# Weight sums of a down projection by transfers in DRAM, moved from the attention phase to the up phase, in a hybrid encoder block on one core

## The chip, the core and the metric

The kernel runs on one core of a Trainium2 chip. The core has five engines, each with an instruction queue of its own that is worked off in order: PE (TensorE, matrix products), DVE (VectorE), ACT (ScalarE), POOL (GpSimd) and SP (SyncE, which here only issues transfers). Sixteen DMA engines move the data of all queues. A transfer that SP or POOL issues is started when the instruction's turn comes and its semaphores are satisfied; until then everything behind it on that queue stands still.

The metric is the device time of one execution in microseconds. Nothing is computed on the host but the layout of the inputs.

## The reference, cut to what matters

One encoder layer with 512 tokens and a model width of 2048, in float32:

```
mod = silu(c) @ w_ada + b_ada;  sh1, sc1, gt1, sh2, sc2, gt2 = split(mod, 6)
h = rms_norm(x, g_mix) * (1 + sc1) + sh1
xr, yr, q, k, v, f = split(h @ w_in)
y_rec = recurrent group(conv, gates, scan over time) * gelu(yr)
y_att = attention of 8 heads with a forget bias, q and k normalised per head
x = x + gt1 * (concat(rms_norm(y_rec), rms_norm(y_att)) @ w_out)
h2 = rms_norm(x, g_ffn) * (1 + sc2) + sh2
gate, up = split(h2 @ w_up)
x = x + gt2 * ((silu(gate) * up) @ w_down)
```

`w_up` is 2048 x 11264 and `w_down` 5632 x 2048. The row gt2 (2048 values) scales the last sum.

## The kernel before, in words

Weights come from HBM in float32. Each weight tile, and each activation, is split into a rounded part (ACT) and a remainder (DVE), and each product is made of three matmuls (high by high, high by low, low by high). The program is written with a tile framework: its scheduler orders the instructions of each engine by their place in the source and by the priorities given (`tc.high_priority(offset=...)` moves a block forward in the order), as soon as data and a buffer are there in its own model of time. The order is fixed when the kernel is built; what the chip then does is to wait, queue by queue. `tc.issue_after(ins)` puts what the block issues behind `ins` on the queue of `ins`, and adds no wait.

The stages follow one another:

- input projections, from 0 to about 190 us;
- the heads (`head_evac`, `attention`, `rec_pair`): the projection of head h+1 runs on PE while hooks between its steps do the attention of head h, a part of the recurrent group and some columns of `w_ada`. Each head's statistics `ss` go through POOL (`rms_rstd`, lines 277 and 280), because the power -1/2 is taken there; `norm` on DVE waits for it, the transposes of q and k on PE wait for `norm`;
- the output projection `wo0` to `wo3` (from about 670 us), then two groups of the up projection, `up0` and `up1` (from 850 us), with the rstd of the new x through POOL;
- the up phase (`for f in range(2 * STD, FT)`, 40 values of f): seven products per f in place of eight, from sums and differences of quarters (a Strassen scheme). Each f has two chunks, c = 0 and 1; a chunk loads 1 MB of weights by two transfers on SP (`fast_chunk`, line 1019). The loads of c = 0 use tag `raw`, those of c = 1 tag `raw2`, with two buffers each. After each chunk, with n = 2 (f - 4) + c, the source calls `gt2_piece` (while n < 64) and `sum2` (for n even, while n < 66). `keep_act` writes the activations to DRAM tiles `td`;
- the down phase: the seven products of a second scheme in four phases (`PHASES`): products 4 and 5, 1 and 7, 6, 2 and 3. Each phase runs over 11 blocks q (`NQ`). `dn_chunk` loads for each product the weight block (`dn_load`, line 1080), 1 MB as two transfers with two buffers of `raw` and two of `raw2`, and the activations (line 1092) into pages `tl`, splits both, and `dn_mm` issues 24 matmuls per q and product.

Some products take sums of weight blocks. `wdn[0..3]` are the four quarters of `w_down`, by q. Product 6 takes `wdn[0] + wdn[2] + wdn[3]`, product 3 the same plus `wdn[1]`; others take a sum of two, made on DVE (line 1099) after the loads. The sum of three is made in DRAM by `sum2`: for n = 0 SP copies `wdn[0, q]` into `s2d[q]` (line 966), for n = 1 and 2 POOL issues two transfers of half a block each that add `wdn[2, q]` and `wdn[3, q]` onto it (line 970). Each waits for the one before it on the same half. Product 3 loads `s2d[q]` and adds the other product's block `wdn[1, q]` on DVE.

Pages are tiles of 128 x 512 from pools by tag: 32 of "h", 16 of "b", 16 of "c", 4 of "d". A page is free for the next user when its last reader is done. In the up phase the transformed inputs T hold all "h" pages and some of the others. In the down phase `tl` and `th` come from "h". In phase 3 the products of the last two q of product 2 are held back (`hold`, lines 1100 to 1109) so that the outputs can be finished one by one; their 16 pages come from "c".

`gt2_spread` brings gt2 from a column layout (`mods[GT2]`, 128 x 16) into rows spread over all partitions: PE transpose, ACT copy, a store of 16 rows to `gt2d` in DRAM (line 1133), and four spreading loads into pages `gt2b` (line 1137), called in phase 2 after q = 2. `finish` (lines 1140 to 1146) loads a piece of x, multiplies and adds on DVE, and stores the outputs that are complete after phase 2; `last_out` does the rest in phase 3.

Of the kernel before, what the change touches and what calls it, by code (L numbers as in the profile page):

```python
# [8 lines left out]
F32 = mybir.dt.float32  # L9
# [5 lines left out]
P = 128  # L15
# [48 lines left out]
def block_kernel(ctx, tc, xT, crow, adaT, vecs, bfr, w1, wyr, wqkv0, wqkv, wgate, wout, wup0, wups, wdn, outT):  # L64
# [16 lines left out]
    def page(name, tag, shape=None):  # L81
        return pgp.tile(shape or [P, S], F32, tag=tag, name=name, bufs=TAGS[tag])

    def acc(name):
        return psa.tile([P, S], F32, tag="acc", name=name)
# [875 lines left out]
        nc.sync.dma_start(out=td[1][q][:, 1, ks], in_=w[:, :HS])  # L961
        nc.sync.dma_start(out=td[2][q][:, 0, ks], in_=w[:, HS:])

    def sum2(q, n):
        if n == 0:
            nc.sync.dma_start(out=s2d[q], in_=wdn[0, q])
        else:
            for i in range(2):
                cs = slice(i * 1024, (i + 1) * 1024)
                nc.gpsimd.dma_start(out=s2d[q][:, cs], in_=wdn[n + 1, q, :, cs], accum_op=ALU.add)  # L970

    def up_out(gi, ps, bup, fs):
        for f in fs:
# [36 lines left out]
    def fast_chunk(f, c):  # L1010

        nm = f"uq{f}_{c}"
        with tc.high_priority(offset=AHEAD):
            if c:
                raw = bp.tile([P, 2048], F32, tag="raw2", name=nm + "r")
            else:
                raw = wp.tile([P, 2048], F32, tag="raw", name=nm + "r", bufs=RAW)
            for i in range(2):
                nc.sync.dma_start(out=raw[:, i * 1024:(i + 1) * 1024], in_=wups[f - 2 * STD, c, :, i * 1024:(i + 1) * 1024])
            blocks = raw.rearrange("p (b m) -> p b m", b=4)  # L1020
            hi, lo = wsplit(raw[:, :1024], 1024, nm + "a")
            out = [(4, hi[:, :512], lo[:, :512]), (1, hi[:, 512:], lo[:, 512:])]
            hi, lo = page(nm + "ch", "d"), page(nm + "cl", "d")
            nc.scalar.activation(R(hi), blocks[:, 3], AF.Copy)
            nc.vector.tensor_sub(R(lo), blocks[:, 3], hi)
            out.append((2, hi, lo))
            nc.vector.tensor_add(blocks[:, 0:3:2], blocks[:, 0:2], blocks[:, 2:3].broadcast_to([P, 2, 512]))  # L1027
            nc.vector.tensor_add(blocks[:, 1], blocks[:, 1], blocks[:, 0])  # L1028
            hi, lo = wsplit(raw[:, :1024], 1024, nm + "s")
            out += [(5, hi[:, :512], lo[:, :512]), (6, hi[:, 512:], lo[:, 512:])]  # L1030
            nc.vector.tensor_add(blocks[:, 3], blocks[:, 3], blocks[:, 1])  # L1031
            hi, lo = wsplit(raw[:, 1024:], 1024, nm + "t")
            out += [(7, hi[:, :512], lo[:, :512]), (3, hi[:, 512:], lo[:, 512:])]
        return out
# [5 lines left out]
    for f in range(2 * STD, FT):  # L1040
        ps = [bank(f + 1, b, f"uf{f}p{b}") for b in range(4)]
        m = {p: ps[b][:, h * HS:(h + 1) * HS] for p, (b, h) in where.items()}
        for c in range(2):
            for p, hi, lo in fast_chunk(f, c):
                for k in range(4):
                    th, tl = T[p][c * 4 + k]
                    ks = slice(k * P, (k + 1) * P)
                    for n, (w, x) in enumerate(((hi, th), (hi, tl), (lo, th))):
                        first, last = c + k + n == 0, c == 1 and k == 3 and n == 2
                        nc.tensor.matmul(m[p], lhsT=R(w[:, ks]), rhs=R(x), start=first and p in opens, stop=last,  # L1050
                                         skip_group_check=True)
            if f == 2 * STD and c == 0:
                up_last()
            n = 2 * (f - 2 * STD) + c
            if n < 4 * KT:
                gt2_piece(n)
            if n < 6 * NQ and n % 2 == 0:
                sum2(n // 6, n // 2 % 3)
        g, u = page(f"ug{f}", "c"), page(f"uu{f}", "c")
        w1_, w2_ = (ap_.tile([P, S], F32, tag="x", name=f"uw{f}_{i}", bufs=2) for i in range(2))  # L1060
        two = lambda t: t.rearrange("p (a b) -> p a b", a=2)
        twice = lambda t: t.unsqueeze(1).broadcast_to(halves)
        nc.scalar.activation(w1_[:, lo_half], m[1], AF.Copy)
        nc.vector.tensor_add(two(g), two(ps[0]), twice(w1_[:, lo_half]))
        nc.vector.tensor_sub(two(w2_), twice(g[:, hi_half]), two(ps[1]))
        nc.vector.tensor_add(g[:, hi_half], m[3], w2_[:, lo_half])
        nc.vector.tensor_sub(u[:, lo_half], m[4], w2_[:, hi_half])
        nc.vector.tensor_sub(u[:, hi_half], m[5], w2_[:, hi_half])
        nc.scalar.activation(g, g, AF.Silu)
        nc.vector.tensor_mul(g, g, u)  # L1070
        keep_act(g, f)

    PHASES = (((4, 3, 1), (5, 2, 0)), ((1, 0, 0), (7, 2, 1)), ((6, -1, 0),), ((2, 1, 0), (3, -1, 1)))

    def dn_load(tag, blk, q, nm):
        pool = wp if tag == "raw" else bp
        raw = pool.tile([P, 2048], F32, tag=tag, name=nm, bufs=RAW)
        src = s2d[q] if blk < 0 else wdn[blk, q]
        for i in range(2):
            nc.sync.dma_start(out=raw[:, i * 1024:(i + 1) * 1024], in_=src[:, i * 1024:(i + 1) * 1024])  # L1080
        return raw

    def dn_chunk(ph, q, hold=False):
        prods = PHASES[ph]
        out = {p: [] for p, _, _ in prods}
        with tc.high_priority(offset=AHEAD):
            raws, ts = [], []
            for n, (p, blk, ix) in enumerate(prods):
                nm = f"dq{p}_{q}"
                raws.append(dn_load("raw2" if n or (len(prods) == 1 and q % 2) else "raw", blk, q, nm + "r"))  # L1090
                tl, th = page(nm + "tl", "h"), page(nm + "th", "h")
                nc.sync.dma_start(out=tl, in_=td[ph][q][:, ix])
                nc.scalar.activation(R(th), tl, AF.Copy)
                nc.vector.tensor_sub(R(tl), tl, th)
                ts.append((th, tl))
            for n, (p, blk, ix) in enumerate(prods):
                nm, raw = f"dq{p}_{q}", raws[n]
                if n:
                    nc.vector.tensor_add(raw, raw, raws[0])
                for k in range(2):  # L1100
                    if hold and n == 0:
                        w = []
                        for i in range(2):
                            src = raw[:, (2 * k + i) * S:(2 * k + i + 1) * S]
                            hi, lo = page(f"{nm}h{k}{i}", "c"), page(f"{nm}l{k}{i}", "c")
                            nc.scalar.activation(R(hi), src, AF.Copy)
                            nc.vector.tensor_sub(R(lo), src, hi)
                            w.append((hi, lo))
                    else:
                        hi, lo = wsplit(raw[:, k * 1024:(k + 1) * 1024], 1024, f"{nm}w{k}")  # L1110
                        w = [(hi[:, i * S:(i + 1) * S], lo[:, i * S:(i + 1) * S]) for i in range(2)]
                    ks = slice(k * HS, (k + 1) * HS)
                    out[p].append((w, ts[n][0][:, ks], ts[n][1][:, ks]))
        return out
# [10 lines left out]
    gt2b = []  # L1125

    def gt2_spread():
        pt = acc("gt2p")
        nc.tensor.transpose(out=pt[:KT, :P], in_=mods[GT2], identity=ident)
        row = page("gt2r", "d")  # L1130
        nc.scalar.activation(row[:KT, :P], pt[:KT, :P], AF.Copy)
        gd = drp.tile([KT, P], F32, name="gt2d")
        nc.sync.dma_start(out=gd, in_=row[:KT, :P])
        gv = gd.rearrange("(a k) p -> a k p", k=4)
        for a in range(4):
            g = page(f"gt2b{a}", "h")
            nc.sync.dma_start(out=g.rearrange("p (k m) -> p k m", k=4), in_=gv[a:a + 1].broadcast_to([P, 4, P]))
            gt2b.append(g)

    def finish(y, tt, a, nm, out=True):  # L1140
        xt = page(nm + "x", "d")
        nc.sync.dma_start(out=xt, in_=x1t[tt, a])
        nc.vector.tensor_mul(y, y, gt2b[a])
        nc.vector.tensor_add(y, y, xt)
        if out:
            nc.sync.dma_start(out=outT[tt][:, a * S:(a + 1) * S], in_=y)

    def last_out(ps, b, z, tt, nm):
        i = b % 2
# [13 lines left out]
    for ph, prods in enumerate(PHASES):  # L1163
# [4 lines left out]
        for q in range(NQ):  # L1168
# [4 lines left out]
            for p, cells in out.items():  # L1173
                for k, cell in enumerate(cells):
                    dn_mm(ps[p], *cell, ALL, q + k == 0, q == NQ - 1 and k == 1)
            if ph == 2 and q == 2:
                gt2_spread()
        if ph == 0:
            q4, q5 = copies(ps[4], "q4_"), copies(ps[5], "q5_")
# [5 lines left out]
                    nc.vector.tensor_add(x_[b], ps[7][b], q5[b])  # L1185
                    nc.vector.tensor_add(q4[b], ps[7][b], q4[b])
        elif ph == 2:
            v = [page(f"dv{b}", "h") for b in range(4)]
            with tc.high_priority(offset=EVAC):
                for b in range(4):  # L1190
                    nc.vector.tensor_add(v[b], ps[6][b], q1[b])
# [80 lines left out]
```

## Time and profile before

| | us |
|---|---|
| median of 3 runs | 2217.03 |
| lowest and highest | 2216.04, 2217.51 |
| the profiled execution | 2223.3 |
| its span, from the first to the last instruction | 2221.6 |
| PE busy in the span | 2064.6 (93%) |
| DVE busy | 1742.0 (78%) |
| ACT busy | 951.7 (43%) |
| POOL busy | 68.3 (3%) |

The profile is one execution, so sums made from it go by its own 2223.3 us, 6.3 above the median of the runs. The page's slices are 55.5 us each; a digit is the busy share in tenths. In lists of waits, a row names who waited, for whom, and then the sum in us, how often, and the longest. A row of a timeline gives start, length, engine (SPq is SP's transfer queue), line, operation, output and input. A transfer's row shows its issue; the time to landing is given separately. Names such as dq_5r or uq_0r leave out buffer numbers, so that dq_5r stands for the weights of q = 5 of any product.

### The profile page before, as it was taken

Reading aid. Unit: us, or ns where it says so; the run is one execution under the profiler, and the core shown is the slowest. Engines: PE = TensorE matmul, PEld = TensorE weight load, DVE = VectorE, ACT = ScalarE, POOL = GpSimd, SP = SyncE. Lnnn points to the kernel's source line nnn. Section 1 sums busy time; section 2 is a strip of 40 time slices with the busy share of each in tenths; the row PEclk is TensorE's granted clock in tenths of the full one; section 3 lists DMA queues with packets and bytes.
Section 4 is the critical chain, followed back from the end, with each engine's and each line's share of the span. In section 5 each row is a group of like instructions: output and inputs, shape, how many; then the busy total and the mean of one; then the engine's idle time right before and its main releaser. Section 6 shows DMA issues by size and latency. Waiting matters only on the chain.

```text
span 2221.6 us, 32358 instructions
## 1 busy us (share of the span) xinstructions
PE 2064.6 (93%) x12538; PEld 1873.0 (84%) x12538; DVE 1742.0 (78%) x2573; ACT 951.7 (43%) x1316; POOL 68.3 (3%) x81
## 2 busy tenths in 40 slices
PE   8999935679999999999999999999999999997898
PEld 6789835568887888889999999999999988886777
DVE  8899513459768867999988888888888877774798
ACT  4433412447644324544444444444444455443443
POOL 0000121110001000000000000000000000000000
PEclk9999967779999999999999999999999999998999
DMA  9989899986766876345644334343334576765684
GB/s 341 332 307 301 283 243 233 263 244 224 239 234 230 284 265 218 106 146 188 194 130 134 131 118 138 119 134 126 129 128 133 172 253 240 245 233 203 221 287 171
DMA packets 163372, 462.14 MB, mean 208 GB/s; under 512 B 17457, under 2 KB 42465, under 8 KB 158946
## 3 DMA queue, kind: packets, MB, share of 16 engines
q1 hardware_dynamic: 156882, 437.00, 57.8%
q0 software_dynamic: 6336, 23.07, 6.0%
q8 instruction: 98, 1.61, 0.3%
q14 instruction: 56, 0.46, 0.1%
HBM read 424.33 MB, written 70.28 MB: 223 GB/s over the span
## 4 chain that ended last, share of the span: by engine, by line
PE 72%; DMA 12%; DVE 11%; issue 3%; POOL 1%; ACT 1%; SPq 1%; DVEq 0%; POOLq 0%; ACTq 0%
DMA s2d<-in_wdn 5%; PE w1p L231 4%; PE dn6p L231 3%; PE dn7p L231 3%; PE dn1p L231 3%; PE dn5p L231 3%; DMA ada<-in_adaT 2%; PE dn4p L231 2%; PE yr1p L231 2%; PE up0p L231 2%; PE wo3p L231 2%; PE wo2p L231 2%; PE wo1p L231 2%; PE yr0p L231 2%; PE wo0p L231 2%
## 5 line engine op out<-in xcount | busy, mean ns | idle before, releaser
L153 DVE SCALAR_TENSOR_TENSOR ada<-ada,c_b 128x1024 f32<-128x1024 f32 x96 | 116.1, 1219 | 107.5 <-DMA ada<-in_adaT 107.3
L226 ACT ACTIVATE uq_0sh<-uq_0r 128x1024 fp32r<-128x1024 f32 x40 | 42.4, 1060 | 116.2 <-DVE uq_0r L1028 112.1
L227 DVE TENSOR_TENSOR uq_0al<-uq_0r,uq_0ah 128x1024 fp32r<-128x1024 f32 x40 | 49.0, 1224 | 39.7 <-ACT uq_0ah L226 38.6
L226 ACT ACTIVATE uq_1sh<-uq_1r 128x1024 fp32r<-128x1024 f32 x40 | 42.4, 1060 | 86.9 <-DVE uq_1r L1028 86.5
L227 DVE TENSOR_TENSOR uq_0tl<-uq_0r,uq_0th 128x1024 fp32r<-128x1024 f32 x40 | 48.9, 1224 | 32.1 <-ACT uq_0th L226 32.1
L226 ACT ACTIVATE uq_0ah<-uq_0r 128x1024 fp32r<-128x1024 f32 x40 | 42.4, 1060 | 69.0 <-DMA td<-tw 25.5
L226 ACT ACTIVATE uq_1ah<-uq_1r 128x1024 fp32r<-128x1024 f32 x40 | 42.4, 1061 | 57.0 <-issue 57.0
L227 DVE TENSOR_TENSOR uq_0sl<-uq_0r,uq_0sh 128x1024 fp32r<-128x1024 f32 x40 | 49.0, 1225 | 16.3 <-ACT uq_0sh L226 16.3
L226 ACT ACTIVATE uq_0th<-uq_0r 128x1024 fp32r<-128x1024 f32 x40 | 42.4, 1060 | 43.9 <-DVE uq_0r L1031 3.2
L181 DVE SCALAR_TENSOR_TENSOR gt<-gt,c_b 128x512 f32<-128x512 f32 x64 | 43.8, 686 | 18.9 <-DMA gt<-in_adaT 18.6
L226 ACT ACTIVATE uq_1th<-uq_1r 128x1024 fp32r<-128x1024 f32 x40 | 42.4, 1059 | 33.7 <-PE uf31p L1050 1.3
L227 DVE TENSOR_TENSOR uq_1tl<-uq_1r,uq_1th 128x1024 fp32r<-128x1024 f32 x40 | 48.9, 1224 | 9.6 <-ACT uq_1th L226 9.6
L231 PE MATMUL w1p<-hph,w1h 128*128 128x512 f32 x128 | 47.6, 400 | 5.8 <-ACT hph L372 5.8
L231 PE MATMUL w1p<-hpl,w1h 128*128 128x512 f32 x128 | 51.0, 398 | 0.1
L231 PE MATMUL w1p<-hph,w1l 128*128 128x512 f32 x128 | 50.8, 397 | 0.0
L1027 DVE TENSOR_TENSOR uq_0r<-uq_0r 128x1024 f32<-128x1024 f32 x40 | 48.7, 1218 | 0.0
L513 DVE TENSOR_TENSOR qk<-qk,ss 128x512 f32<-128x512 f32 x16 | 10.7, 689 | 48.5 <-POOL ss L280 48.5
L227 DVE TENSOR_TENSOR uq_1sl<-uq_1r,uq_1sh 128x1024 fp32r<-128x1024 f32 x40 | 48.7, 1218 | 0.0
L227 DVE TENSOR_TENSOR uq_1al<-uq_1r,uq_1ah 128x1024 fp32r<-128x1024 f32 x40 | 48.6, 1216 | 0.0
L1027 DVE TENSOR_TENSOR uq_1r<-uq_1r 128x1024 f32<-128x1024 f32 x40 | 48.6, 1214 | 0.0
L541 PE MATMUL s<-qkT,qkT 128*128 128x128 f32 (+3 forms) x64 | 25.7, 505 | 22.1 <-DVE nm L546 17.1
L520 PE MATMUL qkt<-ident,qk 128*128 128x128 f32 x64 | 10.1, 310 | 38.4 <-DVE qk L513 38.4
(12773 smaller groups left out, 8254.0 us busy)
## 6 DMA issues: line engine op xcount, KB each, us to landing
ada<-in_adaT SPq DMA_DIRECT2D x128, 512.0 KB, 5.6
uq_1r<-in_wups SPq DMA_DIRECT2D x80, 512.0 KB, 4.3
uq_0r<-in_wups SPq DMA_DIRECT2D x80, 512.0 KB, 4.7
s2d<-in_wdn POOLq DMA_DIRECT2D x44, 512.0 KB, 12.1
adf<-in_adaT SPq DMA_DIRECT2D x32, 512.0 KB, 6.0
gt<-in_adaT SPq DMA_DIRECT2D x64, 256.0 KB, 3.3
x<-in_xT SPq DMA_DIRECT2D x32, 256.0 KB, 5.9
w1r<-in_w SPq DMA_DIRECT2D x32, 256.0 KB, 5.8
```

Source lines behind the costliest of these rows:

```text
L153: nc.vector.scalar_tensor_tensor(out=t, in0=t, scalar=1.0, in1=cs, op0=ALU.mult, op1=ALU.mult, accum_out=ac)
L181: nc.vector.scalar_tensor_tensor(out=t, in0=t, scalar=1.0, in1=c_b[:, r * S:(r + 1) * S], op0=ALU.mult, op1=ALU.mult, accum_out=gt2_acc[:, ...
L226: nc.scalar.activation(R(hi[:, :n]), raw_ap, AF.Copy)
L227: tail_lo.append(nc.vector.tensor_sub(R(lo[:, :n]), raw_ap, hi[:, :n]).ins)
L231: nc.tensor.matmul(ps, lhsT=R(l), rhs=R(r), start=start, stop=stop)
L513: nc.vector.tensor_tensor(z, z, ss[:, 4 * a:4 * a + 4].unsqueeze(2).broadcast_to([P, NT, P]), ALU.mult)
L520: nc.tensor.transpose(out=pt[:, t * P:(t + 1) * P], in_=z[:, t, :], identity=ident)
L541: nc.tensor.matmul(ps[:, :n], lhsT=qT[:, bs], rhs=kT[:, :n], start=True, stop=False)
L1027: nc.vector.tensor_add(blocks[:, 0:3:2], blocks[:, 0:2], blocks[:, 2:3].broadcast_to([P, 2, 512]))
```

## The change

The copies are tied to SP's queue behind the last weight load that the up phase's source has issued so far; a second DRAM tile `s4d` per q takes the sum of four; POOL adds `s2d` onto it. Where before n even called `sum2`, now n = 3, 4, 5, 6 of each six call `sums24`. Product 3 loads `s4d`, and its sum on DVE goes. `gt2_spread` writes `gt2d` straight from the column layout by a transfer with the two axes exchanged, and is called in phase 0. The pages of `gt2b` and `dv` go from "h" to "c", those of the held products from "c" to "h". The stores of `finish` are issued by POOL.

```
+    s4d = [drp.tile([P, 2048], F32, name=f"s4d{q}") for q in range(NQ)]
+    up_loads = []
+
+    def dram_sum(out, src):
+        for i in range(2):
+            cs = slice(i * 1024, (i + 1) * 1024)
+            nc.gpsimd.dma_start(out=out[:, cs], in_=src[:, cs], accum_op=ALU.add)
+
+    def sums24(q, n):
         if n == 0:
-            nc.sync.dma_start(out=s2d[q], in_=wdn[0, q])
+            with tc.issue_after(up_loads[-1]):
+                nc.sync.dma_start(out=s2d[q], in_=wdn[0, q])
+                nc.sync.dma_start(out=s4d[q], in_=wdn[1, q])
+        elif n < 3:
+            dram_sum(s2d[q], wdn[n + 1, q])
         else:
-            for i in range(2):
-                cs = slice(i * 1024, (i + 1) * 1024)
-                nc.gpsimd.dma_start(out=s2d[q][:, cs], in_=wdn[n + 1, q, :, cs], accum_op=ALU.add)
+            dram_sum(s4d[q], s2d[q])
...
-                nc.sync.dma_start(out=raw[:, i * 1024:(i + 1) * 1024], in_=wups[f - 2 * STD, c, :, i * 1024:(i + 1) * 1024])
+                ld = nc.sync.dma_start(out=raw[:, i * 1024:(i + 1) * 1024], in_=wups[f - 2 * STD, c, :, i * 1024:(i + 1) * 1024])
+            up_loads.append(ld.ins)
...
-            if n < 6 * NQ and n % 2 == 0:
-                sum2(n // 6, n // 2 % 3)
+            if 3 <= n < 3 + 6 * NQ and n % 6 in (3, 4, 5, 0):
+                sums24((n - 3) // 6, (n - 3) % 6)
...
-    PHASES = (((4, 3, 1), (5, 2, 0)), ((1, 0, 0), (7, 2, 1)), ((6, -1, 0),), ((2, 1, 0), (3, -1, 1)))
+    PHASES = (((4, 3, 1), (5, 2, 0)), ((1, 0, 0), (7, 2, 1)), ((6, -2, 0),), ((2, 1, 0), (3, -4, 1)))
...
-        src = s2d[q] if blk < 0 else wdn[blk, q]
+        src = {-2: s2d, -4: s4d}[blk][q] if blk < 0 else wdn[blk, q]
...
-                if n:
+                if n and blk >= 0:
                     nc.vector.tensor_add(raw, raw, raws[0])
...
-                            hi, lo = page(f"{nm}h{k}{i}", "c"), page(f"{nm}l{k}{i}", "c")
+                            hi, lo = page(f"{nm}h{k}{i}", "h"), page(f"{nm}l{k}{i}", "h")
...
     def gt2_spread():
-        pt = acc("gt2p")
-        nc.tensor.transpose(out=pt[:KT, :P], in_=mods[GT2], identity=ident)
-        row = page("gt2r", "d")
-        nc.scalar.activation(row[:KT, :P], pt[:KT, :P], AF.Copy)
         gd = drp.tile([KT, P], F32, name="gt2d")
-        nc.sync.dma_start(out=gd, in_=row[:KT, :P])
+        nc.sync.dma_start(out=gd.rearrange("k p -> p k"), in_=mods[GT2])
         gv = gd.rearrange("(a k) p -> a k p", k=4)
         for a in range(4):
-            g = page(f"gt2b{a}", "h")
+            g = page(f"gt2b{a}", "c")
...
-            nc.sync.dma_start(out=outT[tt][:, a * S:(a + 1) * S], in_=y)
+            nc.gpsimd.dma_start(out=outT[tt][:, a * S:(a + 1) * S], in_=y)
...
-            if ph == 2 and q == 2:
+            if ph == 0 and q == 2:
                 gt2_spread()
...
-            v = [page(f"dv{b}", "h") for b in range(4)]
+            v = [page(f"dv{b}", "c") for b in range(4)]
```

More of the change, by code (lines that the diff above doesn't have):

```diff
@@ L962, in keep_act @@
         nc.sync.dma_start(out=td[2][q][:, 0, ks], in_=w[:, HS:])
-    def sum2(q, n):
-        if n == 0:
-            nc.sync.dma_start(out=s2d[q], in_=wdn[0, q])
-        else:
-            for i in range(2):
-                cs = slice(i * 1024, (i + 1) * 1024)
-                nc.gpsimd.dma_start(out=s2d[q][:, cs], in_=wdn[n + 1, q, :, cs], accum_op=ALU.add)
+    s4d = [drp.tile([P, 2048], F32, name=f"s4d{q}") for q in range(NQ)]
[5 more added lines that the diff above has]
+    def sums24(q, n):
+        if n == 0:
+            with tc.issue_after(up_loads[-1]):
[3 more added lines that the diff above has]
+            dram_sum(s2d[q], wdn[n + 1, q])
+        else:
+            dram_sum(s4d[q], s2d[q])
     def up_out(gi, ps, bup, fs):
```

## The prediction, made before the changed kernel was run

> **What bounds the kernel now.** I read the page first, then the busy time by stretches, the list of waits, and the order of the instructions on POOL and SP.
>
> ```profile
> span 2221.6 us, 32358 instructions
> ...
> PE   8999935679999999999999999999999999997898
> ...
> q1 hardware_dynamic: 156882, 437.00, 57.8%
> q0 software_dynamic: 6336, 23.07, 6.0%
> ```
>
> PE is the bound, except in one hole (slices 4 to 8, some 220 to 500 us) and two dents near the end. Those are the places where the change can win; where PE is full it can only lose. The stretches, cut at the points that matter below (columns: length, PE busy, PEld, DVE, ACT, POOL, granted clock, DMA share, GB/s):
>
> ```profile
> 188.83:241.05 52.22, 47.47 (x261) 43.62 (x260) 45.26 (x101) 17.88 (x37) 2.28 (x3) 0.97 0.87 285
> 241.05:486.38 245.33, 146.18 (x698) 132.88 (x696) 93.12 (x174) 74.62 (x140) 42.74 (x51) 0.76 0.98 251
> 486.38:623.69 137.31, 133.68 (x722) 120.98 (x721) 115.19 (x211) 93.87 (x164) 8.24 (x7) 1.00 0.72 235
> 808.00:886.00 78.00, 78.00 (x384) 65.73 (x383) 56.49 (x92) 30.85 (x45) 2.11 (x2) 1.00 0.65 229
> 977.00:1745.00 768.00, 768.00 (x6402) 768.00 (x6402) 663.38 (x908) 321.31 (x381) 0.00 (x0) 1.00 0.43 140
> 2006.63:2080.38 73.75, 60.13 (x254) 49.21 (x254) 37.22 (x38) 26.93 (x30) 0.00 (x0) 0.88 0.61 206
> 2080.38:2221.60 141.22, 126.54 (x540) 101.55 (x539) 124.75 (x143) 57.04 (x69) 0.00 (x0) 0.97 0.68 231
> ```
>
> The first three are cut at POOL's per-head statistics (ss, one per attention head), so their lengths are head times:
>
> ```profile
> 241.05 0.63 POOL L277 TENSOR_SCALAR ss<-ss 128x8 f32<-128x8 f32 x1 [49.86 <-DVE ss L506]
> ...
> 325.81 0.20 POOL L277 TENSOR_SCALAR ss<-ss 128x8 f32<-128x8 f32 x1
> ...
> 413.48 0.20 POOL L277 TENSOR_SCALAR ss<-ss 128x8 f32<-128x8 f32 x1
> ...
> 486.38 1.09 POOL L277 TENSOR_SCALAR ss<-ss 128x8 f32<-128x8 f32 x1 [15.03 <-DVE ss L506]
> ...
> 623.69 1.10 POOL L277 TENSOR_SCALAR ss<-ss 128x8 f32<-128x8 f32 x1 [41.24 <-DVE ss L506]
> ```
>
> Heads 2, 3 and 4 follow after 84.8, 87.7 and 72.9 us, 245.3 in all. The next three take 137.3, that is 45.8 each, with slightly more PE, DVE and ACT instructions. What lies only in the slow stretch are the weight sums s2d, which nothing ties to the down projection that reads them:
>
> ```profile
> L970 POOL DMA_DIRECT2D s2d<-in_wdn x44: 802/823/1216, 257.4 to 470.5; - x44
> ...
> DMA to landing us min/median/max: 7.8/12.1/21.0
> ```
>
> ```profile
> POOL s2d L970 <- DMA s2d<-in_wdn: 137.7, 24, 14.0
> ...
> DVE qk L513 <- POOL ss L280: 48.5, 8, 25.4
> ...
> PE qkt L520 <- DVE qk L513: 38.4, 1, 38.4
> ...
> PE dn6p L231 <- ACT dq_3th L1093: 13.6, 1, 13.6
> ...
> PE dn2p L231 <- ACT dq_0th L1093: 6.6, 1, 6.6
> ```
>
> They hurt twice. The accumulating transfers stand in POOL's queue ahead of ss and wait there for their predecessors (137.7 us); DVE waits for ss, and PE for DVE (38.4 once). And the DMA engines are full (0.98 against 0.72 later), so the heads' own loads come late.
>
> **The change, part by part.**
>
> *Sums out of the attention phase.* All 11 copies go to SP's queue behind the load of up chunk n = 3, 9, ... 63, and the accumulations can only follow their copy. The bytes left between 241 and 486 us: 251 GB/s x 245.3 us = 61.6 MB, less 11 copies of 1.05 MB and 44 accumulations of 0.52 MB (23.07 MB in the queue's row), = 27 MB, under the 32 MB that the clean stretch moves in 137.3 us. So no engine and no transfer would be fuller than there. The head time is between 45.8 and 52.2 us (the head before the sums, beside the bias loads). I take 47.5, near the clean rows: 245.3 - 3 x 47.5 = 102.8 us won; 88.7 to 107.9 from the bounds, and a little more if the 698 matmuls against 722 count.
>
> *The same work, and half as much again, in the up phase.* 66 accumulations instead of 44, 22 copies instead of 11. An accumulation takes 6.0% of 2221.6 us / 44 = 3.03 us of all 16 DMA engines, measured while they were full; a copy of 1.05 MB, at the other queue's rate (57.8% of 2221.6 us for 437 MB, 2.94 us per MB), 3.1. Per set of six chunks (60.5 us, 20.16 per two chunks, 768 us in the window being full) that is 6 x 3.03 + 2 x 3.1 = 24.4 us. The window's own share of 0.43 is 26.0. Together 50.4 of 60.5 us: 0.83, it fits. What covers late weight loads:
>
> ```profile
> 1203.25 0.80 SPq L1019 DMA_DIRECT2D uq_0r<-in_wups  x2
> ```
> ```profile
> 1234.02 1.06 ACT L226 ACTIVATE uq_0ah<-uq_0r 128x1024 fp32r<-128x1024 f32 x1 [1.82 <-PE uf17p L1050]
> ```
> ```profile
> uq_0r<-in_wups SPq DMA_DIRECT2D x80, 512.0 KB, 4.7
> ```
>
> With two buffers per tag a load fills the buffer just freed and is read two f later: issued at 1203.3, read at 1234.0, landing in 4.7. There are 26 us to spare; accumulations under a full DMA landed in 21.0 at worst. The copies wait for nothing, so SP isn't held; POOL is empty here and its waits hold nobody. Cost 0 to 30 us (a load now and then behind two copies); I take 2.
>
> *The first set.* Its pin is the load of uq5_1, which is issued long before the up phase, as the SP row shows; POOL's next duty is the rstd of x1:
>
> ```profile
> 807.75 1.75 SPq L1019 DMA_DIRECT2D uq_1r<-in_wups  x4
> ```
> ```profile
> 878.66 1.10 POOL L277 TENSOR_SCALAR rstd_1t<-rstd_1t 128x4 f32<-128x4 f32 x1 [186.65 <-DVE rstd_1t L293]
> ```
>
> If the copies start at 810, three rounds at 12.1 and some 10 for the copies end near 857, in time. At 21.0 a round they end near 885 to 895, 6 to 17 us late, and PE waits for rstd_1's spread. The stretch 808 to 886 has 35% of 78 us = 27 us of DMA free against 24.4. Cost 0 to 24; I take 4, near the median row.
>
> *Phase 2 and gt2.* The row of gt2 needs a PE transpose and an ACT copy, and its store and spread stand in SP's queue before the activations of phase 2:
>
> ```profile
> 2024.22 0.32 SPq L1133 DMA_DIRECT2D gt2d<-gt2r  x1
> ...
> 2028.07 1.74 SPq L1137 DMA_DIRECT2D gt2b<-gt2d  x4
> 2029.86 0.42 SPq L1092 DMA_DIRECT2D dq_3tl<-td  x1
> ```
> ```profile
> 1886.95 5.44 PE dn1p L231 x24
> ...
> 2024.22 3.78 DMA gt2d<-gt2r
> ```
>
> Phase 2 is 11 q of 5.44 us = 59.8; it takes 73.75. gt2 goes to phase 0 and leaves the "h" pages to the activations (dv too), so I count all 13.9 as won; bounds 8 and 13.9, as the pages held for phase 3 now come out of "h".
>
> In phase 0 the store writes 2048 elements of 4 bytes, and the four spreads behind it on SP wait for its landing, with the loads for q = 4 and later behind them. The nearest rows: 3.78 us for the same 8 KB in 16 rows; at the top one packet per element at the mean of the queue (57.8% x 2221.6 x 16 / 156882 = 131 ns), 128 per engine, 16.8 us plus the 3.78.
>
> ```profile
> 1795.00 1.88 SPq L1080 DMA_DIRECT2D dq_4r<-in_wdn  x2
> ```
>
> Phase 0 ends at 1886.95, so it starts 22 x 5.44 us earlier, at 1767.3, and q = 4 at 1810.8: its second weights lead by 16, less some 5 for landing and 5 for the splits, 6 are free. Cost 0 to 15; I take 1, as packets this small must cost less than the mean one of 2.8 KB.
>
> *Phase 3.* Eleven sums of weights leave DVE:
>
> ```profile
> L1099 DVE TENSOR_TENSOR dq_5r<-dq_5r x3: 2287/2291/2293, 1811.7 to 2140.1; 128x2048 f32<-128x2048 f32 x3
> ```
> ```profile
> 2082.75 0.81 SPq L1080 DMA_DIRECT2D dq_2r<-in_wdn  x2
> 2083.59 0.91 SPq L1092 DMA_DIRECT2D dq_0tl<-td  x2
> ```
> ```profile
> 2206.25 10.89 PE dn2p L231 x48
> ```
>
> 11 x 2.29 = 25.2 us; DVE falls from 124.75 to 99.6 of the stretch, and PE's 22 cells of 5.44 (119.7) become the bound. After the last matmul (2217.14) come 4.5 us. The floor is 124.2 against 141.2, 17.0 to be won. At its start PE waits 6.6 us for dq_0tl, queued behind a weight load that waits for a buffer; more "h" pages let it go earlier. The output stores of `finish` go to POOL, where only one another stand behind them; even at 21.0 us to landing the last is out before the end. I take 10 of 17.0: the finishing work of phase 2 still fills DVE at the start. Bounds 2 and 17.
>
> *Sum*, against the profiled execution of 2223.3: -102.8 - 13.9 - 10 + 2 + 4 + 1 = -119.7, so 2103.6. That execution is 6.3 above the median of the runs, 2217.03; the forecast in their terms is **2097**. Its own range is 2075 to 2125 from the bounds.
>
> The VectorE page of the Trainium skill (VectorE: DVE Perf Modes, The three transpose paths) says that a plain DMA that transposes by strides is 19 times slower than the crossbar's. If that factor fell on the 3.78 us of the row store, the landing would be an estimated 72 us, and the sum 65 us worse; no run here shows it yet, and the page gives no case of 8 KB.
>
> **The rivals.**
>
> (a) *Heads stay slow.* Behind the sums stands another wait: DVE also waits for ada loads, and the bias loads had filled the DMA to 0.87. If the three heads take 57 us, 5 over the worst clean head, 28 are lost: 2125. Against it: 27 MB are left.
>
> (b) *The first set delays rstd_1*: 17 us more than I took, 2114.
>
> (c) *The element store holds SP.* To the top of its bound it is 15 instead of 1: 2111. Beyond that each us of landing is one of PE; 50 us more would give 2161. Against the long form: even a packet as dear as the mean one ends at 20.6. The rule of 19 times, above, speaks for it.
>
> (d) *POOL's issues slow DVE.* 66 issues of 0.82 us = 54 us. If DVE stood still meanwhile and PE with it: 2151. Against it: in the attention phase an op that ran beside the 44 issues kept its time,
>
> ```profile
> L153 DVE SCALAR_TENSOR_TENSOR ada<-ada,c_b x96: 1198/1219/1228, 264.2 to 806.5; 128x1024 f32<-128x1024 f32 x96
> ```
>
> 2% from least to most, and DVE has 105 us free in the up phase. The GPSIMD Engine Reference of the Trainium skill (Specifications) speaks for this rival: GpSimd shares its SBUF interfaces with VectorE and contends with instructions of two SBUF inputs, which are most of those in the up phase.
>
> (e) *Slower than before: the up phase becomes DMA-bound.* Full PE turns into waits for uq loads once the work per set passes 60.5 us, 1.20 times my 50.4; each us beyond costs 11. All 119.7 are eaten at 71.4 per set, 1.42 times. At 1.5 times (75.6) the loss is 166: 2263. For it: 0.43 is measured without any accumulation beside it. Against it: 3.03 is measured in the crowd.
>
> That the sums aren't moved can hardly be: the pin is an order within SP's own queue.
>
> **How the numbers follow.** Forecast 0.68 (2097); (a) 0.10, (b) 0.08, (c) 0.05 (0.01 of it the long form), (d) 0.04, (e) mild, 10 to 110 us lost, 0.02, (e) in full 0.03. The range, 2072 to 2142, holds the forecast and (a) to (c), a few us below the bounds' sum, and leaves out most of (d) and (e). A measurement can tell about 0.2% (4.4 us): faster 0.96, same 0.01, slower 0.03.
>
> **What would show it.** After: no s2d transfer before some 808 us; ss at about 47 us steps throughout; POOL L277 for ss never behind L970; the DMA share of the up phase near 0.8 and PE still full, with uq landings under 20 us; no wait of dn6p for dq_3th; L1099's sums 22 times instead of 33, and DVE near 100 us in phase 3. Wrong: a PE below 9 tenths in the up phase, rstd_1 after 885 us, a gap in phase 0 behind gt2d, or heads 2 to 4 above 52 us each.

## The result, and the profile after

The changed kernel takes 2112.07 us (median of 4 runs, 2102.77 to 2112.49) against 2217.27 before: a ratio of 0.9516, 95% interval 0.949 to 0.9543. Ratios here and below leave out two executions at a lower granted clock, one of `sums_only` (2882 us at 0.65) and one of the kernel before (2279 us at 0.89). Its profiled execution took 2112.08, with a span of 2110.4, so the two spans stand 111.2 apart. The forecast was 2097 in terms of the median and 119.7 less than the profiled execution; the direction and most of the size came. Of the 15 us that the median is off, 8.5 are the change's; the other 6.3 are the distance of the first profiled execution from its median, which the second doesn't have.

The page of the changed kernel: the hole in PE at slices 4 to 8 is gone, and the sums now show as DMA share in the second half of the span.

```profile
span 2110.4 us, 32392 instructions
...
PE   8999999999999999989899999999999999999999
...
DMA  9989766667678962597698876777743587677794
...
q0 software_dynamic: 10144, 36.70, 9.7%
```

What is left of gaps in PE are the two 8s in slices 17 and 19 (counted from 0), about 900 to 1060 us: in the up phase, where PE had been full. The heads, by POOL's statistics as before:

```profile
240.24 0.63 POOL L277 TENSOR_SCALAR ss<-ss 128x8 f32<-128x8 f32 x1 [48.08 <-DVE ss L506]
...
277.51 1.10 POOL L277 TENSOR_SCALAR ss<-ss 128x8 f32<-128x8 f32 x1 [34.92 <-DVE ss L506]
...
320.34 1.10 POOL L277 TENSOR_SCALAR ss<-ss 128x8 f32<-128x8 f32 x1 [39.41 <-DVE ss L506]
...
369.62 1.10 POOL L277 TENSOR_SCALAR ss<-ss 128x8 f32<-128x8 f32 x1 [46.46 <-DVE ss L506]
```

Heads 2 to 4 take 129.4 us instead of 245.3, and each ss is now released by DVE, never by a transfer. The stretches of the changed kernel (columns as in the prediction): heads 2 to 4, the up phase while gt2 is still being computed, the up phase after it, phase 2, phase 3:

```profile
240.24:369.62 129.38, 127.14 (x706) 116.95 (x705) 93.94 (x176) 75.25 (x141) 8.33 (x6) 0.99 0.64 215
...
849.00:1110.00 261.00, 244.37 (x1949) 242.42 (x1950) 222.78 (x347) 97.69 (x121) 14.90 (x18) 0.95 0.76 214
1110.00:1662.00 552.00, 552.00 (x4603) 552.00 (x4602) 462.73 (x602) 230.23 (x274) 34.65 (x42) 1.00 0.68 195
...
1925.00:1984.85 59.85, 59.85 (x265) 49.58 (x265) 39.16 (x43) 29.80 (x34) 0.00 (x0) 1.00 0.72 246
1984.85:2110.40 125.55, 120.71 (x529) 98.50 (x528) 98.06 (x125) 51.80 (x61) 4.43 (x8) 0.99 0.68 239
```

In the second and third row lies the surprise: the same sums cost nothing from 1110 us on, with the DMA engines at 0.68 on average, and 17 us of idle PE and a lower granted clock (0.95) before that. Following the start of each stage through both traces gives where the 111.2 us come from:

| step | us |
|---|---|
| gained up to the third output projection (wo3 starts at 806.8 before, 689.4 after) | -117.4 |
| wo3 to the first fast f (uf4: 957.5, 849.0) | +8.9 |
| uf4 to uf43 (1746.5, 1662.6) | +24.6 |
| end of the up phase and phase 0 (dn1: 1886.8, 1805.4) | +2.5 |
| phase 1 (dn6: 2006.5, 1925.0) | -0.1 |
| phase 2, to the last matmul of product 6 (76.6, 59.9) | -16.7 |
| phase 3 and the end (138.5, 125.6) | -13.0 |

The cut between the last two rows is not that of the prediction. The prediction ended phase 2 of the kernel before at 2080.38, but product 6 still had about a dozen matmuls to go there, and PE's wait for phase 3 began only behind them:

```profile
2082.47 0.61 PE L231 MATMUL dn6p<-dq_10w1h,dq_10tl 128*128 128x512 f32 x2
2089.69 1.22 PE L231 MATMUL dn2p<-dq_0w0h,dq_0th 128*128 128x512 f32 x2 [6.61 <-ACT dq_0th L1093]
```

PE's waits in the changed kernel, the largest that the kernel before did not have:

```profile
PE uf8p L1061 <- DVE uq_0sl L227: 6.3, 1, 6.3
...
PE x1p L901 <- DVE x L871: 4.7, 2, 4.3
PE uf11p L1061 <- DVE uq_0tl L227: 4.7, 1, 4.7
```

In the up phase (uf8, uf11) PE waits for DVE, which splits the up weights; not for a weight load. Of the 24.6 us from uf4 to uf43, 16.6 are idle PE; the other 8.0 are longer busy time, at a granted clock that fell to 0.80, 0.50 and 0.68 in the three stretches of 5 us from 935 to 950, around the longest wait. And DVE, in the list of waits of the changed kernel:

```profile
DVE gt L181 <- DMA gt<-in_adaT: 50.3, 26, 6.6
```

It was 18.6 before (the row of line 181 in the first trace's waits). SP's queue around uf8, and the chain that ended last there:

```profile
903.28 0.81 SPq L1029 DMA_DIRECT2D uq_1r<-in_wups  x2
...
906.69 0.76 SPq L975 DMA_DIRECT2D s2d<-in_wdn  x1
907.49 0.59 SPq L976 DMA_DIRECT2D s4d<-in_wdn  x1
913.32 0.81 SPq L1029 DMA_DIRECT2D uq_0r<-in_wups  x2
914.18 0.92 SPq L171 DMA_DIRECT2D gt<-in_adaT  x2
```
```profile
914.65 11.84 DMA gt<-in_adaT
...
927.25 12.91 DMA gt<-in_adaT
```

A copy pair goes out, then a weight load, then the loads of gt: pieces of 256 KB of `w_ada`, which `gt2_piece` multiplies on DVE. They have two buffers, so a piece is loaded about one piece ahead, and these two land after 11.8 and 12.9 us; the median was 3.3 in the kernel before. The mean share of the DMA engines hides what happens there. In a burst of some 25 us behind the copies they are full, while the set's accumulations run:

```profile
915.00:940.00 25.00, 20.73 (x173) 20.52 (x172) 14.05 (x22) 8.71 (x11) 4.03 (x6) 0.96 0.99 238
```

DVE works in order, so the splits behind the gt step stand too. DVE's last gt step in the kernel before was at 1117.8 us, and up to there it had no slack for that: it was busy 139.3 of 143.9 us in the same stretch (uf4 to uf11) of the kernel before,

```profile
957.50:1101.40 143.90, 143.90 (x1177) 143.90 (x1178) 139.29 (x225) 62.15 (x75) 0.00 (x0) 0.98 0.58 187
```

97%, against the 86% of the whole up phase on which the prediction relied.

### The profile page after: what moved, and what is told of

The parts are those of the page before. It is cut to its first block, busy times and chain, and to the rows that moved or that the text cites. A ratio compares the mean times of both kernels' runs of the same rounds, so it can differ in the third digit from the quotient of the medians.

```text
span 2110.4 us, 32392 instructions
## 1 busy us (share of the span) xinstructions
PE 2050.9 (97%) x12537; PEld 1861.0 (88%) x12537; DVE 1719.2 (81%) x2562; ACT 946.9 (45%) x1315; POOL 93.0 (4%) x111
## 4 chain that ended last, share of the span: by engine, by line
PE 72%; DVE 12%; DMA 10%; issue 3%; ACT 1%; POOL 1%; SPq 1%; DVEq 0%; ACTq 0%
DMA gt<-in_adaT 5%; PE w1p L231 4%; PE dn7p L231 3%; PE dn1p L231 3%; PE dn6p L231 2%; PE yr1p L231 2%; PE wo2p L231 2%; PE wo1p L231 2%; PE dn5p L231 2%; PE yr0p L231 2%; PE wo0p L231 2%; PE dn4p L231 2%; PE up0p L231 2%; PE h2p L231 2%; PE h3p L231 2%
## 5 line engine op out<-in xcount | busy, mean ns | idle before, releaser
L153 DVE SCALAR_TENSOR_TENSOR ada<-ada,c_b 128x1024 f32<-128x1024 f32 x96 | 116.1, 1219 | 29.2 <-DMA ada<-in_adaT 29.0
L226 ACT ACTIVATE uq_1sh<-uq_1r 128x1024 fp32r<-128x1024 f32 x40 | 42.4, 1060 | 89.2 <-DVE uq_1r L1039 86.2
L970 POOL DMA_DIRECT2D s2d<-in_wdn x44 | 36.8, 910 | 743.8 <-DMA s2d<-in_wdn 743.8
L227 DVE TENSOR_TENSOR uq_0sl<-uq_0r,uq_0sh 128x1024 fp32r<-128x1024 f32 x40 | 49.0, 1225 | 16.3 <-ACT uq_0sh L226 16.3
L1080 ACT ACTIVATE ug<-ug 128x512 f32<-128x512 f32 x40 | 25.3, 633 | 63.7 <-DVE ug L1077 63.5
L163 DVE SCALAR_TENSOR_TENSOR ada<-ada,c_b 128x1024 f32<-128x1024 f32 x32 | 39.0, 1217 | 2.6 <-DMA ada<-in_adaT 2.6
```

The costliest lines, as they stand in the source:

```text
L153: nc.vector.scalar_tensor_tensor(out=t, in0=t, scalar=1.0, in1=cs, op0=ALU.mult, op1=ALU.mult, accum_out=ac)
L163: nc.vector.scalar_tensor_tensor(out=t, in0=t, scalar=1.0, in1=c_b[:, cs], op0=ALU.mult, op1=ALU.mult, accum_out=ada_acc[j][:, hf, i:i + 1])
L226: nc.scalar.activation(R(hi[:, :n]), raw_ap, AF.Copy)
L227: tail_lo.append(nc.vector.tensor_sub(R(lo[:, :n]), raw_ap, hi[:, :n]).ins)
L970: nc.gpsimd.dma_start(out=out[:, cs], in_=src[:, cs], accum_op=ALU.add)
```

## The experiments

The theory after the trace: the 33 us lost in the second and third row of the table come from the sets of sums that meet loads with a short lead, gt's above all; the sums' bulk costs nothing. Rival: the sums' traffic itself makes the up weights late. Gains and losses below are read from stage lengths in the profiles, and totals are medians.

### The sums begin when gt is through: late

```
-            if 3 <= n < 3 + 6 * NQ and n % 6 in (3, 4, 5, 0):
-                sums24((n - 3) // 6, (n - 3) % 6)
+            if 21 <= n < 21 + 5 * NQ and (n - 21) % 5 < 4:
+                sums24((n - 21) // 5, (n - 21) % 5)
```

> The changed kernel with one edit: the sets of sums start at chunk n = 21 in place of 3 and come every 5 chunks in place of 6, so that they begin when the 64 gt pieces of w_ada are through. Theory: the lost time lies in DVE's waits for gt loads, which stand behind the copies on SP's queue and have only two buffers; no set meets them now, so the 8 us of up0 and the 24 us of uf8 and uf11 go, 2112 to about 2080, and PE is full from uf4 to uf43. Rival: the sums' traffic itself makes the up weights late; the sets are denser now (24.4 us of transfers in 50.4 us instead of 60.5), so PE loses as much or more, 2105 to 2130.

2082.14 us, ratio 0.9404 (0.938 to 0.9428). The first copies go out at 1022.4 us, after the last gt step of DVE (1005.2). The stretch from uf4 to uf43, a burst of the second set in it, and DVE's wait for gt:

```profile
843.30:1632.00 788.70, 788.70 (x6551) 788.70 (x6552) 683.74 (x943) 330.08 (x394) 54.70 (x66) 1.00 0.75 213
```
```profile
1075.00:1105.00 30.00, 30.00 (x252) 30.00 (x251) 25.09 (x33) 12.23 (x15) 4.95 (x6) 1.00 0.97 235
```
```profile
DVE gt L181 <- DMA gt<-in_adaT: 19.9, 16, 2.7
```

PE is full throughout, with denser sets than in the changed kernel and through bursts in which the DMA engines are as good as full (0.97), and wo3 to uf4 is back to 151.3 us (159.6 in the changed kernel, 150.7 before). The theory's numbers came; the rival's didn't.

### The sums stay, the gt loads go: gt_noload

```
         if n == 0:
             gt2_load(0)
-        if n < 4 * KT - 1:
-            gt2_load(n + 1)
-        t = gt2_src.pop(n)
+            gt2_load(1)
+        t = gt2_src[n % 2]
```

> The changed kernel, sums from n = 3 as there, but only the first two of the 64 pieces of gt2's columns of w_ada are loaded and each DVE step works on one of these again (62 loads of 256 KB are left out, and gt2 is not the reference's); the DVE instructions stay. Theory (gt loads behind the copies hold DVE, and DVE holds PE): the up phase is full, the steps at uf8 and uf11 are gone, 2080 to 2090. Rival (the sums' traffic makes the up weights late): PE still waits 15 us or more in the up phase, above 2100.

2088.49 us, ratio 0.9421 (0.9401 to 0.9442). From uf4 to uf43 PE is busy 790.0 of 790.6 us with the early sets in place:

```profile
841.80:1632.40 790.60, 790.04 (x6554) 788.99 (x6555) 667.36 (x874) 332.82 (x399) 49.55 (x60) 1.00 0.68 195
```

So the sums' traffic alone makes no up weight late: the rival fell. But this is not a clean trial of gt's loads. Without loads to wait for, the scheduler moved all 64 DVE steps of gt ahead of uf4 (614 to 747 us), so the up phase lost gt's work on DVE along with its loads. That it is the loads rests on the waits. In five kernels that keep all 64 loads, DVE waits for gt from uf4 to uf43 for 1.9 us (before), 3.9 (late), 13.1 (`sums_only`), 19.7 (`no_s4d`) and 32.3 (the changed kernel), and the stretch is longer than before by 0, 0, 7.0, 12.7 and 24.6.

The first set's part (wo3 to uf4) did not go: 155.7 us, and PE waits 4.3 us there for DVE's step on x (4.7 in the changed kernel). In late, where no set lies in that stretch, the loss is gone, so the set causes it. Which load it makes late stays open: in the changed kernel's chain from 690 to 750 us three gt loads stand with 10.6, 5.9 and 8.3 us, and DVE waits 5.6 us for up0r, the weights of up0 (1.9 before); in gt_noload the wait for up0r is 4.9 with no gt load near, but DVE had gt's steps to do in that stretch.

### The move alone: sums_only

The sum of three moved and tied, in the kernel before; nothing else. `up_loads` is collected as in the change.

```
+            with tc.issue_after(up_loads[-1]):
                 nc.sync.dma_start(out=s2d[q], in_=wdn[0, q])
...
-            if n < 6 * NQ and n % 2 == 0:
-                sum2(n // 6, n // 2 % 3)
+            if 3 <= n < 3 + 6 * NQ and n % 6 in (3, 4, 5):
+                sum2((n - 3) // 6, (n - 3) % 6)
```

> The kernel before with one part of the change: the sums of three go to n = 3, 4, 5 of each six chunks and are tied behind the up loads; no s4d, no other edit. Theory: the attention phase gains its 117 us whole; the sets are lighter (15 us of transfers instead of 24), so the up phase loses 8 to 25; the down phase stays as before, its stretch from dn6 to the end 215 us: 2217 - 117 + 16 = 2116, between 2108 and 2126. Rival: part of the down phase's gain comes from the move itself, then below 2100.

Ratio 0.9579 (0.9563 to 0.9595), span 2117.7. wo3 starts at 688.7, 118.1 us earlier than before; wo3 to uf4 takes 154.9, 4.2 more than before, and uf4 to uf43 796.0, 7.0 more; from dn6 to the end 217.5 us against 215.1 before. So the attention phase's gain is the move's, and the down phase's is not; the theory held.

### The tie left out: no_pin

```
-            with tc.issue_after(up_loads[-1]):
-                nc.sync.dma_start(out=s2d[q], in_=wdn[0, q])
-                nc.sync.dma_start(out=s4d[q], in_=wdn[1, q])
+            nc.sync.dma_start(out=s2d[q], in_=wdn[0, q])
+            nc.sync.dma_start(out=s4d[q], in_=wdn[1, q])
```

> The changed kernel without the tie of the copies to the up loads; they stand at the same place in the source. Theory (only the tie keeps the sums out of the attention phase): the copies go early again, with 22 more accumulations and 11 more copies, 100 us of transfers more than before, and heads 2 to 4 or more of them take 70 to 95 us each; the down phase keeps its 30: 2190 to 2290. Rival (the later place in the source is enough): within 10 us of the changed kernel.

2239.76 us, ratio 1.011 (1.009 to 1.0131): 1.1% slower than the kernel before, as the theory had it. The accumulations run from 257 us on, as in the kernel before, though the source calls them in the up phase:

```profile
L970 POOL DMA_DIRECT2D s2d<-in_wdn x44: 802/828/1199, 256.6 to 611.8; - x44
L970 POOL DMA_DIRECT2D s4d<-s2d x22: 802/814/1173, 281.4 to 617.8; - x22
```

Five heads from 240.3 us take 372.4, 60 to 81 each. Everything that this change wins beyond the down phase hangs on the line with `issue_after`.

### The sum of four taken back: no_s4d

Product 3 loads s2d and DVE adds, as before; the rest is the changed kernel.

> The changed kernel without the sum of four: product 3 loads s2d and DVE adds the other block, as before; pages, queue and gt2 as changed. Theory: phase 3 is bound by DVE again, and its stretch grows from 125.6 to about 135 us; the sets are lighter, which may give back up to 15 us in the up phase: 2105 to 2122, to be read by the stretch. Rival: phase 3 gained by the pages and POOL's stores, and its stretch stays below 128 us.

2103.25 us, ratio 0.9494 (0.9478 to 0.951), some 8 us less than the changed kernel (0.9528, 0.9514 to 0.9541, in its second trial below). Phase 3:

```profile
1970.10:2101.70 131.60, 122.27 (x529) 98.28 (x528) 118.71 (x135) 51.49 (x61) 4.42 (x8) 1.00 0.66 228
```

131.6 us against 125.6: the 25 us of DVE sums are worth 6 of the 13.0, between theory (10) and rival; the total came below the 2105 expected. The lighter sets lose only 12.7 us from uf4 to uf43 (24.6 in the changed kernel). As placed in this change, the sum of four cost in the up phase more than it gave in phase 3.

### The other parts of the down phase, undone one by one in late

old_gt2: PE transpose and row store, in phase 2, as before.

> Run late with one part undone: gt2's row by PE transpose, ACT copy and row store, in phase 2 after q = 2, as before; the pages stay as changed. Theory (the store and the spreads on SP stand ahead of dq_3tl): phase 2 takes 70 to 75 us again instead of 59.9, total 2082 + 13 = 2095. Rival (the dent came from the shortage of h pages, which let the activations' loads fall behind in SP's order): phase 2 stays below 63 us, total 2080 to 2085.

old_pages: `gt2b` and `dv` in "h", the held products in "c", as before.

> Run late with one part undone: gt2b and dv in h pages, the held products in c pages, as before; gt2 by DRAM in phase 0 stays. Theory: phase 2 stays near 60 us, and the start of phase 3 loses the wait for dq_0tl again, 3 to 7 us, as 8 fewer h pages hold the activations' loads back: 2085 to 2089. Rival (the pages carry phase 2's gain): phase 2 at 70 us or more, 2092 or more.

old_gt2_pages: both together.

> Run late with two parts undone together, gt2 by PE in phase 2 and the page tags as before; each alone left phase 2 at 60 us. Theory (the dent needs both: few h pages put the activations' loads late in SP's order, and the gt2 chain then holds them): phase 2 takes 70 to 75 us again, total 2098 to 2106. Rival (the dent went with the sum of four or POOL's stores): phase 2 at 60 to 63, total near 2089, as with the old pages alone.

out_on_sp: the stores of `finish` by `nc.sync`.

> Run late with one part undone: the stores of finish on SP. Theory: each store waits on SP for DVE and holds the loads behind it; the stretch of phase 3 grows from 125 to 127 to 131 us, total 2084 to 2088. Rival (the stores cost nothing, phase 3 gains only by the DVE sums and the pages): stretch 125 to 126.

| kernel | ratio (95%) | phase 2 | phase 3 |
|---|---|---|---|
| late | 0.9404 (0.938 to 0.9428) | 59.9 | 125.1 |
| old_gt2 | 0.9396 (0.938 to 0.9411) | 59.9 | 128.4 |
| old_pages | 0.9422 (0.9407 to 0.9436) | 59.9 | 138.3 |
| old_gt2_pages | 0.9499 (0.9483 to 0.9514) | 76.5 | 135.7 |
| out_on_sp | 0.9394 (0.9377 to 0.9412) | 59.9 | 128.6 |

Phase 2 ends here with the last matmul of product 6. The theory for old_gt2 fell: gt2 by PE in phase 2 costs phase 2 nothing. The theory for both together held: 76.5 us, as in the kernel before (76.6); the 70 to 75 expected were counted to the earlier cut. SP's queue shows why; first old_gt2, then old_gt2_pages, each in phase 2:

```profile
1905.47 0.38 SPq L1103 DMA_DIRECT2D dq_0tl<-td  x1
1906.41 0.33 SPq L1144 DMA_DIRECT2D gt2d<-gt2r  x1
```
```profile
1912.86 0.32 SPq L1144 DMA_DIRECT2D gt2d<-gt2r  x1
...
1915.99 1.75 SPq L1148 DMA_DIRECT2D gt2b<-gt2d  x4
1917.78 0.42 SPq L1103 DMA_DIRECT2D dq_3tl<-td  x1
```
```profile
PE dn6p L231 <- ACT dq_3th L1104: 13.3, 1, 13.3
```

With pages to spare, the activations of phase 2 are all loaded before gt2's store comes (the row ahead of it is already dq_0tl of phase 3), and the chain delays nobody. With few, the activations from q = 3 on stand behind it. One alone doesn't hurt phase 2; the dent needs both.

In phase 3 the pages are the largest part, 13.2 us where 3 to 7 were expected, with two waits of PE in old_pages that late hasn't:

```profile
PE dn2p L231 <- ACT dq_0th L1104: 6.2, 1, 6.2
...
PE dn3p L231 <- ACT dq_4w0h L226: 2.6, 1, 2.6
```

The two waits are 8.8 of the 13.2 us; the rest isn't traced. The total shows less than the phase: by the ratios old_pages is some 4 us slower than late, and in its profile product 6 starts 4.9 us earlier (1889.1, 1894.0). POOL's stores are worth 3.5 us in the profile of phase 3, old_gt2 loses 3.3 there; in the total neither can be told from late, and late's own phase 3 took 0.9 us more when it was profiled again. The parts overlap (13.2 + 6 + 3.5 + 3.3 is twice the 13.0 won).

### The element store inside phase 0: gt2_in_phase0

```
+        with tc.issue_after(dn_loads[-1]):
             nc.sync.dma_start(out=gd.rearrange("k p -> p k"), in_=mods[GT2])
```

`dn_loads` collects the loads of `dn_load`, as `up_loads` does.

> Run late with the element store of gt2 tied on SP behind the last weight load of phase 0 that the source has issued by q = 2, so that it and the four spreads run inside phase 0 and not in the up phase. Theory (the bound of the prediction): landing 8 to 15 us as in the changed kernel (13.7), SP held that long, 6 of it hidden, phase 0 longer by 3 to 10 us, total 2085 to 2092. Rival (a store of 2048 elements is tens of us): phase 0 longer by 30 or more. Second rival: nothing, the loads lead far enough.

2088.18 us, ratio 0.942 (0.9406 to 0.9434). Phase 0 takes 130.4 us against 123.4 in late, 7 more, within the theory. In the changed kernel the scheduler had put the store at 1077.9 us, in the up phase, where nothing waited; only its four spreads run in phase 0. The two rows of transfers, of the changed kernel and of this one (KB each, us to landing):

```profile
gt2d<-mod SPq DMA_DIRECT2D x1, 8.0 KB, 13.7
```
```profile
gt2d<-mod SPq DMA_DIRECT2D x1, 8.0 KB, 14.2
```

### The two versions on one chip: after_again, late_again

> The changed kernel once more, on the chip that also runs late: 2102 to 2113, as before.

> Run late once more, on the same chip as the changed kernel: 2079 to 2084, that is 1.2 to 1.5% below the changed kernel, intervals apart. If the gain of late were a matter of the chip it ran on, the two would be within 0.4%.

2111.51 us, ratio 0.9528 (0.9514 to 0.9541), and 2081.29, ratio 0.9388 (0.9375 to 0.9401), against the same runs of the kernel before. The version that beats both is late: 1.4% below the changed kernel, 6.1% below the kernel before.

## Why the prediction came out as it did

The direction, the source of the gain and the tie were right. That the total lies 8.5 us from the forecast is in part luck: the wins came out 20.5 us larger than forecast and the costs 29.0 larger. The stated 2125 does not follow from the bounds either; with every term at its upper bound the sum is 2187.

**Sums out of the attention phase: right in mechanism, mis-sized.** Forecast -102.8 with a bound of 107.9; 115.9 came between the same two heads (245.3 to 129.4), 117.4 up to wo3. I priced a head at 47.5 us, near the next clean heads. The stretch had fewer matmuls (698 against 722); scaled by them, the 137.3 us of the clean stretch would be 132.7, and 112.6 won. The row was on the table, and I called it "a little more". The last 3.3 us stay open. Part of them may be the profiled execution of the kernel before, 6.3 above its median: its other stages up to phase 1 agree with those of the later profiles to about 1 us, so an excess would lie in the slow heads, but no run here shows it. sums_only shows that the gain is the move's, no_pin that it hangs on the tie.

**The up phase: the step that failed is "Cost 0 to 30 us; I take 2".** 24.6 came. The capacity sum held (from 1110 us on no PE time is lost at a share of 0.68, in late none at 0.75), and the weight loads kept their cover: landing 20.0 us at worst against 26 to spare, and PE never waited for one. But I had asked only what covers the up weights, and not what else loads there. gt's loads have a lead of one piece, and DVE, whose 105 us to spare in (d) are a mean over the phase (86% busy), is at 97% while gt runs. late removes the loss by moving the sums, gt_noload by taking gt's loads, and with them its DVE steps, out of the phase. Rival (e), a phase bound by DMA, did not come: in late the sets come every five chunks, and PE is busy 788.7 of 788.7 us.

**The first set: 8.9 against 4, by another way than I had.** rstd_1 on POOL was not held: POOL issued the set's last accumulation at 729.9 and was idle until 769.5. The delay fell on loads of that stretch, above; rstd_1 only came later with them. So (b) names nearly the measured total, 2114, but by luck: its mechanism did not occur.

**gt2 in phase 0: 2.5 against 1**, and not by the store, which ran in the up phase. What the 2.5 are stays open. Tied into phase 0 the store costs 7, inside the 0 to 15 that I gave it, and neither (c) nor its long form came.

**Phase 2: -16.7 against -13.9.** The 73.75 us that I read stop 2.7 short of product 6's last matmul, so 16.7 were to be won, more than my bound of 13.9, and all of it came. Half of the reason is right: the chain of gt2 on SP was the last wait, but it was harmful only because the lack of pages had put the activations behind it. In late, either edit alone wins it.

**Phase 3: -13.0 against -10.** Within the bounds, though the same cut put 2.7 us too many into what I counted as its 17.0. I put the DVE sums first; they are 6, the pages 13, in trials that overlap.

**(d), POOL's issues slowing DVE, does not show.** A split of DVE with two inputs in SBUF, in the changed kernel:

```profile
L227 DVE TENSOR_TENSOR uq_0sl<-uq_0r,uq_0sh x40: 1218/1225/1228, 842.7 to 1661.8; 128x1024 fp32r<-128x1024 f32 x40
```

The longest is 0.8% over the shortest, beside 66 issues on POOL (the operation shown in the prediction varied by 2.5%, 1198 to 1228, not 2); the medians of this operation before (1225) and after are equal.

Sum of the misses: the attention phase gave 14.6 more than forecast (with the 1.5 up to wo3), phase 2 2.8 and phase 3 3.0; the up phase cost 22.6, the first set 4.9 and phase 0 1.5 more.

## What to carry to other kernels

When work is moved under another stage, list every load that the stage issues with its lead, the smallest buffers first, and take the busy share of the in-order engine, and of the DMA engines, in the stretch where they run, not over the stage. In no_pin the scheduler placed the transfers that wait for nothing more than 700 us ahead of the stage whose source calls them; the order on their own queue kept them where they were wanted. Two edits that each remove a wait can be the same gain: undo them singly and together before crediting either.

## What was not expected of the hardware

A store of 8 KB as 2048 elements of 4 bytes landed in 13.7 and 14.2 us, against 3.8 as 16 rows in the kernel before: a factor of 3.6 to 3.7. The factor of 19 that the VectorE page of the Trainium skill (VectorE: DVE Perf Modes, The three transpose paths) gives for strided transposes with a large innermost stride at the destination is against the crossbar's transpose, and none ran here; what the measurement decides is that the 72 us worked out from it for this store did not come.

In the bursts of a set the DMA engines are full (0.99 from 915 to 940 us), and two loads of 256 KB took 11.8 and 12.9 us to land, against a median of 3.3 in the kernel before. The second was issued at 927.2, some 10 us after the set's two copies had landed (7.6 and 9.5 us after 906.7 and 907.5), so it isn't their place ahead of it on SP's queue; what ran beside it were the accumulations that POOL issues.
